# Spreading norm factors by transposes, a shorter wait behind the third f group, and an early word of weight tile two

## The chip, the cores and the metric

The kernel runs on one core of one Trainium2 chip. The metric is the device time in microseconds of one execution; a figure for a kernel is the median of several executions. All inputs and outputs are float32.

## The reference

The kernel computes a two-layer bidirectional encoder trunk over 256 tokens of width 2048. Sixteen learned meta tokens are put in front, so that every stage works on T = 272 tokens. Each layer does this:

```python
h = rmsnorm(x, norm_mix[i])                       # x * rsqrt(mean(x*x) + 1e-6) * g
q, k, v, f, ga, gf = split(h @ w_in[i])           # 1024, 256, 256, 1024, 2048, 2048 columns
q, k = rope_2d(rmsnorm(q, q_norm[i])), rope_2d(rmsnorm(k, k_norm[i]))   # per head of 128
attn = softmax(q @ k.T / sqrt(128)) @ v           # 8 heads, 2 key/value heads
four = real(fft2(f, axes=(positions, 128 channels of a group)))          # 8 groups, ortho
merged = sigmoid(ga + b) * (attn @ w_attn_br[i]) + sigmoid(gf + b) * (four @ w_four[i])
x = x + merged @ w_out[i]
h2 = rmsnorm(x, norm_ffn[i])
u_gate = dwconv3(h2 @ w_up_gate)                  # 5632 channels, 3 taps along the tokens
x = x + (silu(u_gate) * (h2 @ w_up_val)) @ w_down[i]
```

The meta tokens are dropped at the end. Two small quantities matter here: the norm factor of each token (one number for each of the 272 tokens, the reciprocal root of a mean of squares), and the same factor for each token and key head.

## The kernel before

**Data layout.** Activations are held with channels on the partitions and tokens along the free axis: `XT` is the residual stream, 16 blocks of 128 channels by 272 tokens. A factor per token must therefore be the same on all 128 partitions when it multiplies such a block. `rstdB` is that: 128 x 272, the norm factors spread over all partitions.

**Matmuls.** Each weight matrix is streamed in tiles of 128 x 1024 f32 (512 KB, tag `raw`). Each tile is split in two parts of the reduced format fp32r: the high part `wh` is a cast on ScalarE (L286) and the low part `wl` a subtraction on VectorE (L288). The activations are split in the same way (`xHL`; L501 and the operation behind it). A product is then three matmuls, high by high, high by low and low by high (L357 to L359 in `group`, L424 to L426 in `first_groups`). One group has 256 output channels: two accumulators in PSUM over 64 weight blocks of 128 x 128.

**The order of the work.** SP issues the loads of weight tiles in the order of a list, a few tiles ahead. TensorE runs through the groups. Everything that is not such a matmul (norms, the Fourier branch, attention, gates) is written as Python generators that are pushed on a list called `shadow`. After every second pair of weight blocks, `step()` resumes the first generator whose pause has run out; the number that a generator yields is its pause in steps. So `yield 4` puts at least four steps of matmuls between two parts of a side job on TensorE. `drain()` resumes the generators there and then until none is left, and `until(hold, flag)` does so until a flag is set. Within this order a scheduler places the instructions; the loads marked `keep_in_program_order`, and TensorE and VectorE inside `manual_schedule`, stay as written.

**The norm factors** (`norm_stats`). The sums of squares `acc` lie with one partial sum on each partition. Three transposes against an identity (L590, `ps_nst`) and a reduction give one number per token, with the tokens on the partitions: column 0 for the 16 meta tokens (repeated on all partitions), columns 1 and 2 for the two blocks of 128 tokens. A power of -1/2 on GpSimd gives `tok`, 128 x 3 (L497). To spread them, three VectorE operations multiply the columns into a constant mask of identities (`dg`, L600), and a plain f32 matmul with a matrix of ones (L603, `ps_nb`) sums over the partitions, so that every output partition holds all 272 factors; ScalarE copies them to `rstdB`. `kstats` does the same for each of the two key heads (`dk`, L966 `ps_kb`). `norm_stats` is run four times, `kstats` twice.

**The start.** GpSimd fills small tiles with constants; ScalarE's queue loads the norm gains `prm`; SP issues the first blocks of `XT` and of weight tile one (`raw0`) by turns. Weight tile two (`raw1`) is held back on purpose: a one-column copy on GpSimd reads the first block of `raw0` and writes `raw1`, and the load of `raw1` has to wait for that copy.

```python
nc.gpsimd.tensor_copy(raws[1][:, 0, 0:1], r0[:, 0, 0:1])                            # L469
tc.keep_in_program_order(nc.sync.dma_start(raws[1], chunks[1][0]))                  # L470
tc.keep_in_program_order(nc.sync.dma_start(XT[:, 4:8, :], xT[:, 4:8, :]))
```

Behind it SP issues tiles three and four (`load_raw`) and `XT` 8:12, and, after the first matmuls, `XT` 12:16 and a part of the constants.

**The f groups of layer 0.** The first two f groups run together (`first_groups`, `ps_f`), and beside them the generator `sums` forms the norm factors. It then evicts the two groups with `f_evac`: VectorE multiplies each accumulator by `rstdB` and folds the positions into `E` (L654, L655; the middle positions into `remE` and `remO`). Each eviction pushes a generator `f_chan(i)`, the transform over channels: four matmuls `ps_fa` (L674, L675) that read `E`, and the copies behind them. Then:

```python
ps = group((l, "f", 2), xr(0), T, "aux")
drain()
f_evac(2, ps)
...
f_evac(3, group((l, "f", 3), xr(0), T))
```

Of the kernel before, what the change touches and what calls it, by code (L numbers as in the profile page):

```python
# [76 lines left out]

C_COS, C_SIN, C_MASK = 0, T, 2 * T
C_ID = 3 * T
C_CC = C_ID + P  # L80
# [15 lines left out]
def _constants():  # L96
# [11 lines left out]
    eye = np.eye(P)  # L108
    m16 = (np.arange(P)[:, None] % NM == np.arange(NM)[None, :]) / (P // NM)
    mask = np.concatenate([m16, eye, eye], 1)  # L110
    j = np.arange(P)
# [14 lines left out]
    gm = (np.arange(P)[:, None] // NM == np.arange(NG)[None, :]).astype(np.float64)  # L126
    consts = np.concatenate([cos, sin, mask, eye, cc, sc, br, gm], 1).astype(f32)
    bmat = np.concatenate([b0, b1], 1).astype(f32)
# [27 lines left out]
def encoder_kernel(ctx, tc, xT, params, consts, bmat, cfold, csign, w_fl, w_f64c, w_in, w_abr, w_four, w_f64, w_out, w_up, w_down, w_vn, w_dn, w_dt, out):  # L156
# [163 lines left out]
    def drain():  # L320
        while shadow:
            step(True)
# [77 lines left out]
    def first_groups(pss):  # L400
# [4 lines left out]
        for kt in range(KT // CW * 2 * CW):  # L405
# [26 lines left out]
            if kt == 0:  # L432
                tc.keep_in_program_order(nc.sync.dma_start(XT[:, 12:16, :], xT[:, 12:16, :]))
                tc.keep_in_program_order(nc.sync.dma_start(cst[:, C_MASK:C_CC], consts[:, C_MASK:C_CC]))
            step()
# [7 lines left out]
    cst = per.tile([P, C_N], F32, name="cst")  # L443
    ones = per.tile([P, P], F32, name="ones")
    warm = per.tile([P, 1], F32, name="warm")
# [12 lines left out]
    small = ctx.enter_context(tc.tile_pool(name="small", bufs=4))  # L458

    nc.gpsimd.memset(mhalf, -0.5)  # L460
    nc.scalar.dma_start(prm[:, 0:P_BG], params[:, 0:P_BG])
# [13 lines left out]
    tc.keep_in_program_order(nc.sync.dma_start(XT[:, 8:12, :], xT[:, 8:12, :]))  # L475
    nc.gpsimd.memset(ones, 1.0)
    nc.gpsimd.memset(V3.bitcast(F32), 0.0)
# [6 lines left out]
    sin = cst[:, C_SIN:C_SIN + T]  # L484
    mask = cst[:, C_MASK:C_MASK + T]
    ident = cst[:, C_ID:C_ID + P]
# [70 lines left out]
    def weight_sums():  # L557
# [7 lines left out]
        for s_ in range(1, len(VSETS)):  # L565
# [6 lines left out]
            for q, base, more in kinds:  # L572
                for j in range(NV // 2 + 1):
# [3 lines left out]
                    if j:  # L577
                        issue(dst(q, j - 1), more(j - 1), accum_op=ALU.add, max_dma_last_dim=4096)
                        ready_sums.update((s_, q, 2 * j - 2 + k) for k in range(2))
                        yield 1  # L580

    def norm_stats(holder, gap=0):
        am = small.tile([P, P // NM, NM], F32, tag="am", name="am", bufs=1)
        nc.vector.tensor_copy(am, _rep(acc[:, 0:NM], P // NM))
        lhs = (am.rearrange("p a b -> p (a b)"), acc[:, 16:144], acc[:, 144:272])
        if gap:
            yield gap
        ps = psum.tile([P, 512], F32, tag="aux", name="ps_nst")
        for i in range(3):
            nc.tensor.transpose(ps[:, i * P:(i + 1) * P], lhs[i], ident)  # L590
        ms = small.tile([P, 3], F32, tag="ms", name="ms")
        nc.vector.tensor_reduce(ms, ps[:, 0:3 * P].rearrange("p (i n) -> p i n", i=3), axis=AX.X, op=ALU.add)
        nc.vector.tensor_scalar(ms, ms, 1.0 / D, EPS, op0=ALU.mult, op1=ALU.add)
        tok = small.tile([P, 3], F32, tag="tok", name="tok")
        pow_half(tok, ms)
        holder["tok"] = tok
        yield 4
        dg = small.tile([P, T], F32, tag="sq", name="dg", bufs=2)
        for i, (a, b) in enumerate(BLK):
            nc.vector.tensor_scalar(dg[:, a:b], mask[:, a:b], tok[:, i:i + 1], None, op0=ALU.mult)  # L600
        yield 2
        pb = psum.tile([P, 512], F32, tag="aux", name="ps_nb")
        nc.tensor.matmul(pb[:, :T], ones, dg, start=True, stop=True)  # L603
        nc.scalar.copy(rstdB, pb[:, :T])
        tok2 = small.tile([P, 3], F32, tag="tok2", name="tok2")
        nc.vector.tensor_tensor(tok2, tok, tok, op=ALU.mult)
        holder["tok2"] = tok2
# [4 lines left out]
    for l in range(DEPTH):  # L612
# [6 lines left out]
        with tc.tile_pool(name=f"mix{l}", bufs=1) as mp:  # L619
# [105 lines left out]
            if l == 0:  # L725
                def sums(pss):
                    for m in range(KT):
                        norm_sum(m)
                        yield 4 if m % 4 == 3 else 1
                    yield from norm_stats(hold, 4)  # L730
                    yield 3
                    for i in range(2):
                        f_evac(i, pss[i])
                        yield 2

                pss = []
                push(sums(pss), 4)
                first_groups(pss)
                for dst, src in ((cst[:, 0:C_MASK], consts[:, 0:C_MASK]), (cst[:, C_CC:], consts[:, C_CC:]), (prm[:, P_BG:], params[:, P_BG:])):
                    tc.keep_in_program_order(nc.sync.dma_start(dst, src))  # L740
# [3 lines left out]
                with tc.manual_schedule(engines={mybir.EngineType.PE, mybir.EngineType.DVE}):  # L744
                    ps = group((l, "f", 2), xr(0), T, "aux")
                drain()
                f_evac(2, ps)
# [203 lines left out]
            def kstats():  # L951
# [8 lines left out]
                for kv in range(NKV):  # L960
                    dk = ut("dk")
                    for i, (a, b) in enumerate(BLK):
                        nc.vector.tensor_scalar(dk[:, a:b], mask[:, a:b], rk[:, kv, i:i + 1], None, op0=ALU.mult)
                    yield 5
                    pk = psum.tile([P, 512], F32, tag="aux", name="ps_kb")
                    nc.tensor.matmul(pk[:, :T], ones, dk, start=True, stop=True)  # L966
                    nc.vector.tensor_tensor(kp[:, kv, :], kp[:, kv, :], pk[:, :T], op=ALU.mult)
# [606 lines left out]
```

## Time and profile before

| | before |
|---|---|
| device time, median of 3 runs | 2528.14 us (2527.78 to 2528.75) |
| the profiled execution: device time | 2528.75 us |
| its span in the trace | 2526.8 us (1.95 us lie around it) |
| TensorE (PE) busy | 2516.0 us, 100% of the span, 18848 matmuls |
| VectorE (DVE) busy | 1985.9 us, 79% |
| ScalarE (ACT) busy | 1343.6 us, 53% |
| GpSimd (POOL) busy | 205.7 us, 8% |
| moved by DMA | 706.85 MB, 280 GB/s in the mean |

The span runs from the first to the last instruction in the trace, and the device time has a little more around it. Busy times are times in which an engine runs at least one instruction; matmuls on TensorE overlap, so that a busy TensorE isn't idle, but a matmul's duration is not what it costs. In a row of the timeline the first number is the start in microseconds from the start of the span, the second the duration; then come the engine, the line of the kernel, the operation, the output and the inputs by their names in the program, the shapes, and in brackets the idle time ahead of it with what ended it. In a row of groups, three numbers with slashes are the shortest, the median and the longest duration in ns.

### The profile page before, as it was taken

The numbers are of one execution on the slowest core, as the hardware profiler recorded it, in microseconds if no ns is written. First come the engines' busy times: TensorE is split into PE (matmuls) and PEld (weight loads), VectorE is DVE, ScalarE is ACT, GpSimd is POOL, SyncE is SP. The second block draws the span as 40 slices with busy tenths as digits, with TensorE's granted clock in tenths as the row PEclk, the third lists the DMA queues.
The fourth block names the chain that finished last, engine by engine and source line by source line (L and its number), as shares of the span: only waits on it lengthen the run. The fifth ranks groups of instructions, "written<-read, shape, count | busy, mean of one in ns | idle before, by whom it ended". The sixth has DMA issues, their size and how long they took to land.

```text
span 2526.8 us, 47925 instructions
## 1 busy us (share of the span) xinstructions
PE 2516.0 (100%) x18848; PEld 2433.3 (96%) x18848; DVE 1985.9 (79%) x3151; ACT 1343.6 (53%) x1921; POOL 205.7 (8%) x393
## 2 busy tenths in 40 slices
PE   8999999999999999999999999999999999999999
PEld 8999999999999999999999999999988899998887
DVE  7687866778878667888768887666778787898898
ACT  5455434554444334444445555444676665666665
POOL 0000000012212222222200000000000000000000
PEclk9999999999999999999999999999999999999999
DMA  7545558879999999999975647888778887788887
GB/s 255 165 151 163 190 190 249 260 250 371 395 325 381 397 379 377 384 378 388 379 286 193 204 149 235 269 257 270 245 261 290 296 290 237 259 280 292 277 302 269
DMA packets 194770, 706.85 MB, mean 280 GB/s; under 512 B 22112, under 2 KB 27360, under 8 KB 194288
## 3 DMA queue, kind: packets, MB, share of 16 engines
q1 hardware_dynamic: 146768, 517.09, 59.2%
q0 software_dynamic: 46336, 184.57, 21.2%
q8 instruction: 147, 2.41, 0.4%
q10 hardware_dynamic: 1440, 2.13, 0.2%
q14 instruction: 79, 0.65, 0.1%
HBM read 623.32 MB, written 111.15 MB: 291 GB/s over the span
## 4 chain that ended last, share of the span: by engine, by line
PE 98%; DMA 1%; DVE 0%; ACT 0%; issue 0%; SPq 0%; POOL 0%; DVEq 0%; ACTq 0%
PE ps_p L1414 14%; PE ps_ug L359 7%; PE ps_ug L358 7%; PE ps_ug L357 7%; PE ps_d L358 4%; PE ps_uv L358 4%; PE ps_d L357 3%; PE ps_uv L359 3%; PE ps_d L359 3%; PE ps_uv L357 3%; PE ps_o L358 3%; PE ps_ga L358 2%; PE ps_gf L358 2%; PE ps_o L357 2%; PE ps_ga L359 2%; PE ps_o L359 2%
## 5 line engine op out<-in xcount | busy, mean ns | idle before, releaser
L286 ACT CAST wh<-raw 128x1024 fp32r<-128x1024 f32 (+1 forms) x961 | 999.8, 1046 | 905.8 <-PE ps_ug L358 213.5
L288 DVE TENSOR_TENSOR wl<-raw,wh 128x1024 fp32r<-128x1024 f32 (+1 forms) x961 | 1158.9, 1217 | 407.6 <-ACT wh L286 396.7
L358 PE MATMUL ps_ug<-xHL,wh 128*128 128x272 f32 (+1 forms) x1408 | 401.5, 285 | 0.0
L357 PE MATMUL ps_ug<-xHL,wh 128*128 128x272 f32 (+1 forms) x1408 | 400.8, 285 | 0.0
L359 PE MATMUL ps_ug<-xHL,wl 128*128 128x272 f32 (+1 forms) x1408 | 400.4, 286 | 0.0
L358 PEld LDWEIGHTS ps_ug<-xHL,wh 128*128 128x128 f32 x1408 | 264.7, 188 | 3.2
L357 PEld LDWEIGHTS ps_ug<-xHL,wh 128*128 128x128 f32 x1408 | 264.6, 188 | 3.2
L359 PEld LDWEIGHTS ps_ug<-xHL,wl 128*128 128x128 f32 x1408 | 264.0, 188 | 1.5 <-DVE wl L288 1.1
L1414 PE MATMUL ps_p<-wh,opnd 128*128 128x512 f32 x816 | 222.8, 393 | 0.0
L358 PE MATMUL ps_uv<-xHL,wh 128*128 128x272 f32 x704 | 203.3, 289 | 0.0
L358 PE MATMUL ps_d<-gHL,wh 128*128 128x272 f32 x704 | 202.9, 288 | 0.0
L357 PE MATMUL ps_d<-gHL,wh 128*128 128x272 f32 x704 | 202.9, 288 | 0.0
L359 PE MATMUL ps_uv<-xHL,wl 128*128 128x272 f32 x704 | 202.6, 288 | 0.0
L357 PE MATMUL ps_uv<-xHL,wh 128*128 128x272 f32 x704 | 202.3, 287 | 0.0
L359 PE MATMUL ps_d<-gHL,wl 128*128 128x272 f32 x704 | 202.1, 287 | 0.0
L1414 PEld LDWEIGHTS ps_p<-wh,opnd 128*128 128x128 f32 x816 | 148.4, 188 | 29.6 <-ACT wh L286 0.2
L357 PE MATMUL ps_ga<-xHL,wh 128*128 128x272 f32 (+1 forms) x512 | 147.8, 289 | 0.0
L518 DVE TENSOR_TENSOR wi<-wi,wi 128x512 f32<-128x512 f32 x224 | 147.0, 685 | 0.0
L357 PE MATMUL ps_gf<-xHL,wh 128*128 128x272 f32 (+1 forms) x512 | 146.8, 287 | 0.0
L358 PE MATMUL ps_o<-mL,wh 128*128 128x272 f32 (+1 forms) x512 | 146.5, 286 | 0.0
L358 PE MATMUL ps_ga<-xHL,wh 128*128 128x272 f32 (+1 forms) x512 | 146.1, 285 | 0.0
L359 PE MATMUL ps_o<-mH,wl 128*128 128x272 f32 (+1 forms) x512 | 146.1, 285 | 0.0
(378 smaller groups left out, 5965.7 us busy)
## 6 DMA issues: line engine op xcount, KB each, us to landing
raw<-in_w_up SPq DMA_DIRECT2D x288, 512.0 KB, 6.1
raw<-in_w_in SPq DMA_DIRECT2D x191, 512.0 KB, 4.2
raw<-in_w_down SPq DMA_DIRECT2D x88, 512.0 KB, 7.0
wi<-in_w_dn POOLq DMA_DIRECT2D x80, 512.0 KB, 9.3
ft<-wi POOLq DMA_DIRECT2D x80, 512.0 KB, 7.9
raw<-ft SPq DMA_DIRECT2D x80, 512.0 KB, 4.5
raw<-in_w_out SPq DMA_DIRECT2D x64, 512.0 KB, 4.3
raw<-fv SPq DMA_DIRECT2D x64, 512.0 KB, 4.6
```

Source lines behind the costliest of these rows:

```text
L286: nc.scalar.copy(h[:, a:b], r[:, a:b])
L288: nc.vector.tensor_tensor(lo[:, a:b], r[:, a:b], h[:, a:b].bitcast(F32), op=ALU.subtract)
L357: nc.tensor.matmul(o, h[:, c, sl], a, start=kt == 0, stop=False)
L358: nc.tensor.matmul(o, h[:, c, sl], b, start=False, stop=False)
L359: nc.tensor.matmul(o, lo[:, c, sl], a, start=False, stop=kt == nk - 1)
L518: tt = lambda *v, **kw: tc.keep_in_program_order(nc.vector.tensor_tensor(*v, **kw))
L1414: nc.tensor.matmul(ps[h], x, w[:, 512 * h:512 * h + 512], start=fresh and (s_, q) in BEGIN and first, stop=(s_, q) in END and end, skip_gr ...
```

## The change

There are three edits.

1. *Spread by transposes.* The new `spread(ps, cols)` makes three transposes on TensorE. Each takes one column of the factors, repeated 128 times along the free axis with a step of zero (no copy is made), and transposes it against the identity into 16 or 128 columns of PSUM; the result has the same row on every partition. It takes the place of `dg` and the matmul with ones in `norm_stats`, and of `dk` and its matmul in `kstats`. The pauses are kept (`yield 4` and `yield 2` become `yield 6`; in `kstats` both stay). The tile `ones` and its memset on GpSimd go, and so does the mask among the constants: the early load of constants has 128 columns in place of 400.
2. *The third f group.* `sums` sets a flag once the first two evictions are issued, and behind the third f group `until(hold, "evac")` takes the place of `drain()`. What `drain()` forced out at this place besides, the channel transforms of groups 0 and 1, is left to the steps of the fourth group.
3. *A word per partition of tile two.* The first instruction on GpSimd is now a load of 128 words, the first of each partition of weight tile two, into the first column of `remE`. Nobody reads them: the memset of `remE` writes over them. In the built program that memset has to wait until the words have landed, and it stands on GpSimd right ahead of the copy L469.

In the built program two more things move, by the scheduler and not by an edit: at the start of the last layer's feed-forward part some transposes of the residual stream stand ahead of `ps_nb`, and a few weight casts on ScalarE and folding steps of the weights change places with their neighbours.

```diff
--- before.py
+++ after.py
@@ -75,8 +75,8 @@
 TH = T // 2 + 2
 BLK = ((0, 16), (16, 144), (144, 272))
 
-C_COS, C_SIN, C_MASK = 0, T, 2 * T
-C_ID = 3 * T
+C_COS, C_SIN = 0, T
+C_ID = 2 * T
 C_CC = C_ID + P
 C_SC = C_CC + HC1
 C_BR = C_SC + HC1
@@ -106,8 +106,6 @@
     cos = np.concatenate([np.cos(ar), np.cos(ar), np.cos(ac), np.cos(ac)], 0)
     sin = np.concatenate([-np.sin(ar), np.sin(ar), -np.sin(ac), np.sin(ac)], 0)
     eye = np.eye(P)
-    m16 = (np.arange(P)[:, None] % NM == np.arange(NM)[None, :]) / (P // NM)
-    mask = np.concatenate([m16, eye, eye], 1)
     j = np.arange(P)
     ang = 2.0 * np.pi * ((j[:, None] * j[None, :]) % P) / P
     cc = (np.cos(ang) / math.sqrt(P))[:, :HC1]
@@ -124,7 +122,7 @@
     br[9:16, 1] = sl[129:136, :TH]
     br = np.tile(br.reshape(NM, 2 * TH), (NG, 1))
     gm = (np.arange(P)[:, None] // NM == np.arange(NG)[None, :]).astype(np.float64)
-    consts = np.concatenate([cos, sin, mask, eye, cc, sc, br, gm], 1).astype(f32)
+    consts = np.concatenate([cos, sin, eye, cc, sc, br, gm], 1).astype(f32)
     bmat = np.concatenate([b0, b1], 1).astype(f32)
     return np.ascontiguousarray(consts), np.ascontiguousarray(bmat)
 
@@ -431,7 +429,7 @@
                 pump(len(chunks))
             if kt == 0:
                 tc.keep_in_program_order(nc.sync.dma_start(XT[:, 12:16, :], xT[:, 12:16, :]))
-                tc.keep_in_program_order(nc.sync.dma_start(cst[:, C_MASK:C_CC], consts[:, C_MASK:C_CC]))
+                tc.keep_in_program_order(nc.sync.dma_start(cst[:, C_ID:C_CC], consts[:, C_ID:C_CC]))
             step()
 
 
@@ -441,7 +439,6 @@
     xH, xL = xHL[:, :, 0, :], xHL[:, :, 1, :]
     prm = per.tile([P, P_N], F32, name="prm")
     cst = per.tile([P, C_N], F32, name="cst")
-    ones = per.tile([P, P], F32, name="ones")
     warm = per.tile([P, 1], F32, name="warm")
     mhalf = per.tile([P, 24], F32, name="mhalf")
     BH = per.tile([P, 2, TH], F32R, name="BH")
@@ -457,6 +454,7 @@
     o64m = per.tile([P, P], F32, name="o64m")
     small = ctx.enter_context(tc.tile_pool(name="small", bufs=4))
 
+    nc.gpsimd.dma_start(remE[:, 0, 0:1], chunks[1][0][:, 0, 0:1])
     nc.gpsimd.memset(mhalf, -0.5)
     nc.scalar.dma_start(prm[:, 0:P_BG], params[:, 0:P_BG])
     nc.scalar.activation(warm, mhalf[:, 0:1], AF.Copy)
@@ -473,7 +471,6 @@
     load_raw(3)
     st["raw"] = 4
     tc.keep_in_program_order(nc.sync.dma_start(XT[:, 8:12, :], xT[:, 8:12, :]))
-    nc.gpsimd.memset(ones, 1.0)
     nc.gpsimd.memset(V3.bitcast(F32), 0.0)
     nc.gpsimd.memset(o64.bitcast(F32), 0.0)
     nc.gpsimd.memset(o64m, 0.0)
@@ -482,7 +479,6 @@
 
     cos = cst[:, C_COS:C_COS + T]
     sin = cst[:, C_SIN:C_SIN + T]
-    mask = cst[:, C_MASK:C_MASK + T]
     ident = cst[:, C_ID:C_ID + P]
     ccm = cst[:, C_CC:C_CC + HC1]
     scm = cst[:, C_SC:C_SC + HC1]
@@ -579,6 +575,11 @@
                         ready_sums.update((s_, q, 2 * j - 2 + k) for k in range(2))
                         yield 1
 
+    def spread(ps, cols):
+        for i, (a, b) in enumerate(BLK):
+            n = b - a
+            nc.tensor.transpose(ps[:, a:b], cols[0:n, i:i + 1].to_broadcast([n, P]), ident[0:n, 0:n])
+
     def norm_stats(holder, gap=0):
         am = small.tile([P, P // NM, NM], F32, tag="am", name="am", bufs=1)
         nc.vector.tensor_copy(am, _rep(acc[:, 0:NM], P // NM))
@@ -594,13 +595,9 @@
         tok = small.tile([P, 3], F32, tag="tok", name="tok")
         pow_half(tok, ms)
         holder["tok"] = tok
-        yield 4
-        dg = small.tile([P, T], F32, tag="sq", name="dg", bufs=2)
-        for i, (a, b) in enumerate(BLK):
-            nc.vector.tensor_scalar(dg[:, a:b], mask[:, a:b], tok[:, i:i + 1], None, op0=ALU.mult)
-        yield 2
+        yield 6
         pb = psum.tile([P, 512], F32, tag="aux", name="ps_nb")
-        nc.tensor.matmul(pb[:, :T], ones, dg, start=True, stop=True)
+        spread(pb, tok)
         nc.scalar.copy(rstdB, pb[:, :T])
         tok2 = small.tile([P, 3], F32, tag="tok2", name="tok2")
         nc.vector.tensor_tensor(tok2, tok, tok, op=ALU.mult)
@@ -732,18 +729,19 @@
                     for i in range(2):
                         f_evac(i, pss[i])
                         yield 2
+                    hold["evac"] = True
 
                 pss = []
                 push(sums(pss), 4)
                 first_groups(pss)
-                for dst, src in ((cst[:, 0:C_MASK], consts[:, 0:C_MASK]), (cst[:, C_CC:], consts[:, C_CC:]), (prm[:, P_BG:], params[:, P_BG:])):
+                for dst, src in ((cst[:, 0:C_ID], consts[:, 0:C_ID]), (cst[:, C_CC:], consts[:, C_CC:]), (prm[:, P_BG:], params[:, P_BG:])):
                     tc.keep_in_program_order(nc.sync.dma_start(dst, src))
                 bt = rt("bt")
                 bt = bt[:, :, :TH]
                 tc.keep_in_program_order(nc.sync.dma_start(bt, bmat.rearrange("p (a b) -> p a b", a=2)))
                 with tc.manual_schedule(engines={mybir.EngineType.PE, mybir.EngineType.DVE}):
                     ps = group((l, "f", 2), xr(0), T, "aux")
-                drain()
+                until(hold, "evac")
                 f_evac(2, ps)
                 nc.scalar.copy(BH, bt)
                 tc.keep_in_program_order(nc.vector.tensor_tensor(BL, bt, BH.bitcast(F32), op=ALU.subtract))
@@ -958,12 +956,9 @@
                 pow_half(rk.rearrange("p a b -> p (a b)"), kss.rearrange("p a b -> p (a b)"))
                 yield 6
                 for kv in range(NKV):
-                    dk = ut("dk")
-                    for i, (a, b) in enumerate(BLK):
-                        nc.vector.tensor_scalar(dk[:, a:b], mask[:, a:b], rk[:, kv, i:i + 1], None, op0=ALU.mult)
                     yield 5
                     pk = psum.tile([P, 512], F32, tag="aux", name="ps_kb")
-                    nc.tensor.matmul(pk[:, :T], ones, dk, start=True, stop=True)
+                    spread(pk, rk[:, kv])
                     nc.vector.tensor_tensor(kp[:, kv, :], kp[:, kv, :], pk[:, :T], op=ALU.mult)
                 yield 3
                 qs = swap(kp)
```

## The prediction

> **What bounds the kernel now.** I read the page first, then the waits of TensorE, then the timeline around each edited line.
>
> ```profile
> PE 2516.0 (100%) x18848; PEld 2433.3 (96%) x18848; DVE 1985.9 (79%) x3151; ACT 1343.6 (53%) x1921; POOL 205.7 (8%) x393
> ...
> PE 98%; DMA 1%; DVE 0%; ACT 0%; issue 0%; SPq 0%; POOL 0%; DVEq 0%; ACTq 0%
> ```
>
> TensorE is busy for 2516.0 of 2526.8 us and carries 98% of the chain that ended last. A microsecond counts only if it is taken out of TensorE's own stream or out of a wait of TensorE. The list of those waits is short (columns: us in total, times, longest):
>
> ```profile
> PE ps_f L424 <- ACT wh L286: 5.5, 2, 5.0
> PE ps_fa L675 <- ACT w L368: 1.0, 1, 1.0
> PE ps_uv L354 <- DVE wl L288: 0.7, 2, 0.4
> ```
>
> Of the 5.5 us, 5.0 are the wait for the first data and 0.5 the wait for weight tile two. So all that is idle after the start is about 2.2 us. VectorE at 79% and ScalarE at 53% are on the path nowhere else. That sets the scale: this change can gain some microseconds of TensorE's work and of these waits, not more. I take 0.2%, or 5.06 us of 2528.14, as about what a measurement of this kernel can tell from no change; an edit of 2 us lies inside it.
>
> **Part A, the spread by transposes.** Removed: four matmuls `ps_nb` and four `ps_kb` in plain f32 with 272 columns (each is two records), and 24 small VectorE operations (`dg`, `dk`). Added: 8 times 3 transposes of 16, 128 and 128 columns. A duration is no price on a pipelined engine; the price is how far the starts of the neighbours move apart.
>
> ```profile
> 35.01 0.29 PE L359 MATMUL ps_f<-xHL,wl 128*128 128x272 f32 x1
> 35.14 0.27 PE L590 MATMUL ps_nst<-cst,am 128*128 128x128 f32 x1
> 35.25 0.38 PE L590 MATMUL ps_nst<-cst,acc 128*128 128x128 f32 x2
> ...
> 35.59 0.29 PE L358 MATMUL ps_f<-xHL,wh 128*128 128x272 f32 x1
> ...
> 39.86 0.29 PE L359 MATMUL ps_f<-xHL,wl 128*128 128x272 f32 x1
> 39.99 0.62 PE L603 MATMUL ps_nb<-dg,ones 128*128 128x272 f32 x2
> ...
> 40.57 0.29 PE L358 MATMUL ps_f<-xHL,wh 128*128 128x272 f32 x1
> ```
>
> Undisturbed, neighbours start 0.125 us apart (39.86 and 39.99). Around `ps_nb` the starts of L359 and L358 are 0.71 us apart where two steps would be 0.25, so one f32 matmul costs 0.46 us. Around the three transposes of `ps_nst`, the nearest rows for the new ones (f32, against the same identity), they are 0.58 apart, so three cost 0.33 us, 0.11 each. The saving is 0.13 each time, 8 x 0.13 = 1.05 us. No row shows a stationary operand that is one column repeated, or a transpose of 16 columns. From below: if the short one costs nothing, the gain is 8 x 0.24 = 1.9 us. From above: if each costs its whole duration, there is a loss (a rival below). I take 1.05, the row of the same kind.
>
> ```profile
> L590 PE MATMUL ps_nst<-cst,acc x8: 272/272/273, 35.2 to 1825.3; 128*128 128x128 f32 x8
> ```
> ```profile
> L600 DVE TENSOR_SCALAR dg<-cst,tok x12: 233/279/394, 38.3 to 1828.9; 128x128 f32<-128x128 f32 x8, 128x16 f32<-128x16 f32 x4
> ```
> ```profile
> 36.51 1.80 POOL L497 TENSOR_TENSOR tok<-ms,mhalf 128x3 f32<-128x3 f32 x1 [32.31 <-DVE ms L593]
> ```
>
> The 24 VectorE operations of some 0.28 us are 6 us of an engine with slack: nothing. The new transposes wait for `tok` on POOL, ready at 38.31, and the pauses kept hold their place on TensorE (39.99), so that wait stays covered by 1.7 us. The constants load behind the first matmuls shrinks from 200 to 64 KB; none of TensorE's waits names it: nothing.
>
> **Part B, the third f group.** Before, `drain()` put the channel transforms of groups 0 and 1 (`ps_fa`) into TensorE's stream ahead of the fourth group's matmuls; one of them ran into VectorE.
>
> ```profile
> 44.96 0.33 PE L675 MATMUL ps_fa<-cst,E 128*128 128x65 f32 x2
> ...
> 46.23 0.29 PE L357 MATMUL ps_f<-xHL,wh 128*128 128x272 f32 x1
> 47.47 0.41 PE L675 MATMUL ps_fa<-cst,E 128*128 128x65 f32 x2 [0.96 <-ACT w L368]
> ```
> ```profile
> 46.91 0.42 DVE L654 TENSOR_TENSOR E<-ft 128x254 f32<-128x254 f32 x1
> 47.24 0.42 DVE L655 TENSOR_TENSOR E<-ft 128x256 f32<-128x256 f32 x1
> ```
>
> The starts are 1.24 us apart instead of 0.125: 1.1 us lost. The row names the cast on ScalarE, but what the transform reads is `E`, finished by L654 at 47.33, just before 47.47. With the wait for two evictions alone, the transforms are left to the fourth group's own steps: in the order of the changed program the first comes 24 matmuls later and the second 34 after that, so about 47.9 and 53. The first `E` was ready by 44.96, where its transform ran without a wait, the second is at 47.66, so neither waits. Their own work is unchanged. What is late next: the third eviction now stands ahead of them on VectorE, and one low-half split of the weights moves forward by about 3.5 us, before it is due. Taken: the whole 1.1 us. Its other end is 0, if the stall returns at another place.
>
> **Part C, a word per partition of tile two.** POOL now issues first of all a transfer of 128 words into `remE`; the memset of `remE` waits for its landing, and behind that memset stands the copy L469 that lets SP load weight tile two. Behind that load SP holds XT 4:8, tiles three and four, and XT 8:12, so any delay passes to all of them.
>
> ```profile
> 0.74 0.12 POOL L460 MEMSET mhalf<- 128x24 f32 x1 [0.29 <-POOLq L1566]
> ...
> 2.84 0.50 POOL L1011 MEMSET pn<- 128x128 f32 x3
> 4.02 0.18 POOL L469 COPY raw<-raw 128x1 f32<-128x1 f32 x1 [0.68 <-DMA raw<-in_w_in]
> ...
> 371.76 0.71 POOL L563 DMA_DIRECT2D fv<-in_w_vn  x1
> ```
> ```profile
> 4.23 5.44 DMA raw<-in_w_in
> ```
> ```profile
> 9.75 1.14 ACT L286 CAST wh<-raw 128x512 fp32r<-128x512 f32 x2 [1.23 <-DMA raw<-in_w_in]
> 11.24 1.76 ACT L501 ACTIVATE xHL<-XT,prm 128x272 fp32r<-128x272 f32 x4 [0.34 <-DMA XT<-in_xT]
> 12.91 1.13 ACT L286 CAST wh<-raw 128x512 fp32r<-128x512 f32 x2
> ```
> ```profile
> fv<-in_w_vn POOLq DMA_DIRECT2D x12, 6.6
> ...
> prm<-in_params ACTq DMA_DIRECT2D x1, 32.0 KB, 3.0
> ...
> raw<-in_w_in SPq DMA_DIRECT2D x191, 512.0 KB, 4.2
> ```
>
> When do the words land? The issue costs POOL 0.7 us (371.76 is its first transfer before). The early load of `prm`, 32 KB from ScalarE's queue, took 3.0 us to land; the slow end is 6.6, for POOL's own transfers of 1 MB. I take 3.0, since the words too move almost nothing, and add that 0.7: landed at 0.74 + 3.7 = 4.4. POOL's other memsets, 0.4 us later than now (0.7 less the memset of `ones` and the moved one, 0.14 each), end at 3.8 and hide most of it. Then the memset (0.2) and the copy (0.2): tile two is issued at 4.85 instead of 4.23. It then took 5.44 us, against a median of 4.2 for its group, which I put down to the loads ahead of it. At the median it lands at 9.05, earlier than now (9.67); at 5.44 it lands at 10.3, and TensorE loses 0.6. The touch of the same rows can only help between these. On the gain side the bound is the wait for tile two, 0.5 us in the waits (0.67 by the starts), and little of it can be kept: the next tile's cast at 12.91 stands behind four activations that wait for XT 4:8. Between +0.6 and -0.67 I take -0.1.
>
> By the Trainium skill (DMA: Bandwidth & Descriptors, section Anatomy of one DMA, SWDGE path) such a transfer has a fixed cost of about 2.0 us; as an estimate the words would land at 2.8 and the sum would be the same, with no delay at all. No run here shows it.
>
> **The last layer.** The order there changes a little: row transposes come ahead of `ps_nb`, and ScalarE's weight casts are spread otherwise. The waits there were 0.7 us (L354, above). ScalarE has one cast more (1.14 us by L286 above) queued ahead of another, so I count 0 and keep +1.1 for the range.
>
> **The sum.** -1.05 - 1.1 - 0.1 = -2.25 us. The profiled execution took 2528.75 us (span 2526.8 and 1.95 around it), 0.61 over the median of the three runs. It becomes 2526.5, and the median of 2528.14 becomes **2525.9 us**.
>
> **The rivals.**
> - *The words hold tile two* (slower than before; chance 0.1). If they land after 6.6 us, at 7.34, SP issues at 7.75, 3.5 us late, and with it all that stands behind on SP. TensorE then stands still after tile one for 3.5 us more: 2528.14 - 2.15 + 3.5 = 2529.5. It eats the other parts from a landing at 6.0 on: issued at 6.45, tile two lands after 5.44 us at 11.9, 2.2 later than now. For it: nothing but POOL's big transfers. Against: theirs are a megabyte.
> - *Transposes cost their duration* (slower; 0.04). Three times 0.272 us is 0.82 against 0.46: +0.36 x 8 = 2.9 instead of -1.05, so 2528.14 + 2.9 - 1.1 - 0.1 = 2529.8. Against: the same row starts every 0.11 us. The Trainium skill (TensorE: Matmul & The Clock Gate, Part 4: PE-mode transpose) gives about 275 ns for one in a kernel and would have the clock gate not count it as work. The trace agrees with the duration, 272, but not that it is the price.
> - *Tile two comes earlier and the next tile with it* (0.15). The whole 0.67 is kept: 2525.3.
> - *The stall of part B returns elsewhere* (0.1), so that the move of the transforms does not do what it says: 2527.0. For it: the two operations of `E` start 0.33 us apart and last 0.42, so VectorE is full there. Against: both `E` are done before their new places.
> - *The last layer's cast is late* (0.09): 1.1 us more there, 2527.0.
>
> **How the numbers follow.** The forecast keeps 0.52. Its own ends, a 16-column transpose that costs nothing (-0.85) and tile two late (+0.7), give 2525.0 to 2526.6. The range takes in the three rivals of the same sign, their sums with each other, and half a microsecond for the spread of single runs (2527.78 to 2528.75): 2524.0 to 2528.6. It leaves out the two slow rivals and the joint ends. Faster by over 0.2% needs 2523.08, where all gains at their ends (1.9 + 1.1 + 0.67) still fall short by 1.4: 0.05. Slower by over 0.2% needs 2533.2, both slow rivals at once: 0.02. Within: 0.93.
>
> **What would show each step.** The three transposes should move their neighbours apart by 0.33 us or less. The wait of `ps_fa` should be gone, with no wait of its size between 44 and 60 us. The copy L469 should start at 4.0 to 4.7, and TensorE's wait before 10.4 should be no longer than now. I am wrong if TensorE's waits in the first 15 us grow by over 1 us, if a spread costs over 0.46, or if the span changes where no edited line stands.

## The result, and the profile after

| | before | after |
|---|---|---|
| device time, median of 17 runs each | 2528.49 us (2527.17 to 2530.95) | 2533.01 us (2532.49 to 2535.55) |
| the profiled execution: device time, span | 2528.75, 2526.8 us | 2532.53, 2530.8 us |

The changed kernel is slower: ratio 1.0018, 95% interval 1.0011 to 1.0024, or 4.5 us. The forecast was 2525.9 us in a range of 2524.0 to 2528.6.

The first part of the page of the changed kernel, and its list of TensorE's waits (us in total, times, longest):

```profile
PE 2521.3 (100%) x18856; PEld 2439.4 (96%) x18856; DVE 1982.1 (78%) x3127; ACT 1343.1 (53%) x1921; POOL 204.5 (8%) x393
```
```profile
PE ps_f L422 <- ACT wh L284: 4.9, 2, 4.5
PE ps_uv L352 <- DVE wl L286: 0.3, 1, 0.3
PE ps_p L1409 <- ACT wh L284: 0.2, 1, 0.2
```

The waits fell from 7.2 to 5.4 us, and the wait of `ps_fa` is gone. Yet the span grew by 4.0: TensorE is busy for 5.3 us more, with eight records more. So the time isn't lost in a wait. Where it is lost shows when the two traces are laid side by side, matmul by matmul. At 60 us each matmul starts 1.2 us earlier than before. From there the lead melts: 0.8 us are left at 530 us, in the gate, up and value groups it turns into a lag (+0.5 at 846, +1.6 at 1207 us), in the `d` groups between nothing changes, and at 2489 us it is 3.7. No line of the diff stands there. The view of busy time by stretches shows it as well: in 260 us of the first layer's `ps_ug` and `ps_uv`, and in 100 us of its `ps_d` (columns: us, PE busy with its matmuls, granted clock, DMA share, GB/s). First the kernel before:

```profile
570.00:830.00 260.00, 260.00 (x2077) 1.00 0.98 368
860.00:960.00 100.00, 100.00 (x799) 1.00 1.00 386
```

and the changed kernel:

```profile
570.00:830.00 260.00, 260.00 (x2069) 1.00 0.97 367
860.00:960.00 100.00, 100.00 (x799) 1.00 1.00 383
```

TensorE is busy without a gap in all four, at the same granted clock. In the first stretch it gets through 2069 matmuls instead of 2077 (125.7 ns each instead of 125.2), in the second through the same 799.

Then the edited places. A spread in the timeline of TensorE, changed kernel (the answer to the rows at 39.86 to 40.57; start, duration):

```profile
39.74 0.29 PE L357 MATMUL ps_f<-xHL,wl 128*128 128x272 f32 x1
39.96 0.59 PE L581 MATMUL ps_nb<-cst,tok 16*128 16x16 f32 x3
40.30 0.37 PE L355 MATMUL ps_f<-xHL,wh 128*128 128x272 f32 x1
40.51 0.29 PE L356 MATMUL ps_f<-xHL,wh 128*128 128x272 f32 x1
```

The neighbours (L357 and L356) start 0.77 us apart, against 0.71 around the old matmul and 0.58 around `ps_nst`. The channel transforms moved, and their first matmuls stand in the same timeline without a wait:

```profile
47.95 0.33 PE L672 MATMUL ps_fa<-cst,E 128*128 128x65 f32 x2
...
51.85 0.33 PE L672 MATMUL ps_fa<-cst,E 128*128 128x65 f32 x2
```

And GpSimd's start in the timeline, with the row of the words' load from the list of DMA issues (KB, us from issue to landing):

```profile
1.29 0.73 POOL L457 DMA_DIRECT2D remE<-in_w_in  x1 [0.84 <-POOLq L1561]
...
5.15 0.20 POOL L477 MEMSET remE<- 128x128 f32 x1 [0.81 <-DMA remE<-in_w_in]
5.30 0.17 POOL L467 COPY raw<-raw 128x1 f32<-128x1 f32 x1
```
```profile
remE<-in_w_in POOLq DMA_DIRECT2D x1, 0.5 KB, 3.8
```

### The profile page after: what moved, and what is told of

The parts are those of the page before. It is cut to its first block, busy times and chain, and to the rows that moved or that the text cites. A ratio compares the mean times of both kernels' runs of the same rounds, so it can differ in the third digit from the quotient of the medians.

```text
span 2530.8 us, 47907 instructions
## 1 busy us (share of the span) xinstructions
PE 2521.3 (100%) x18856; PEld 2439.4 (96%) x18856; DVE 1982.1 (78%) x3127; ACT 1343.1 (53%) x1921; POOL 204.5 (8%) x393
## 4 chain that ended last, share of the span: by engine, by line
PE 99%; DVE 0%; ACT 0%; DMA 0%; issue 0%; SPq 0%
PE ps_p L1409 14%; PE ps_ug L356 7%; PE ps_ug L357 7%; PE ps_ug L355 7%; PE ps_uv L355 4%; PE ps_d L356 4%; PE ps_uv L356 3%; PE ps_uv L357 3%; PE ps_d L355 3%; PE ps_d L357 3%; PE ps_gf L355 2%; PE ps_o L356 2%; PE ps_gf L356 2%; PE ps_ga L356 2%; PE ps_ga L355 2%; PE ps_ga L357 2%
## 5 line engine op out<-in xcount | busy, mean ns | idle before, releaser
L286 DVE TENSOR_TENSOR wl<-raw,wh 128x1024 fp32r<-128x1024 f32 (+1 forms) x961 | 1158.5, 1217 | 410.4 <-ACT wh L284 399.1
L356 PE MATMUL ps_ug<-xHL,wh 128*128 128x272 f32 (+1 forms) x1408 | 402.0, 286 | 0.0
L357 PE MATMUL ps_ug<-xHL,wl 128*128 128x272 f32 (+1 forms) x1408 | 400.3, 285 | 0.0
L356 PEld LDWEIGHTS ps_ug<-xHL,wh 128*128 128x128 f32 x1408 | 265.0, 188 | 3.1
L357 PEld LDWEIGHTS ps_ug<-xHL,wl 128*128 128x128 f32 x1408 | 264.8, 189 | 1.1 <-DVE wl L286 0.6
L356 PE MATMUL ps_uv<-xHL,wh 128*128 128x272 f32 x704 | 203.0, 288 | 0.0
L356 PE MATMUL ps_d<-gHL,wh 128*128 128x272 f32 x704 | 202.9, 288 | 0.0
L357 PE MATMUL ps_uv<-xHL,wl 128*128 128x272 f32 x704 | 202.7, 288 | 0.0
L357 PE MATMUL ps_d<-gHL,wl 128*128 128x272 f32 x704 | 202.1, 287 | 0.0
L355 PE MATMUL ps_gf<-xHL,wh 128*128 128x272 f32 (+1 forms) x512 | 147.4, 288 | 0.0
L356 PE MATMUL ps_o<-mL,wh 128*128 128x272 f32 (+1 forms) x512 | 146.6, 286 | 0.0
L356 PE MATMUL ps_gf<-xHL,wh 128*128 128x272 f32 (+1 forms) x512 | 146.2, 286 | 0.0
L356 PE MATMUL ps_ga<-xHL,wh 128*128 128x272 f32 (+1 forms) x512 | 146.2, 286 | 0.0
```

Of the source, the lines that this page charges most:

```text
L286: nc.vector.tensor_tensor(lo[:, a:b], r[:, a:b], h[:, a:b].bitcast(F32), op=ALU.subtract)
L355: nc.tensor.matmul(o, h[:, c, sl], a, start=kt == 0, stop=False)
L356: nc.tensor.matmul(o, h[:, c, sl], b, start=False, stop=False)
L357: nc.tensor.matmul(o, lo[:, c, sl], a, start=False, stop=kt == nk - 1)
```

## The experiments

**What else differs.** The instructions of the `ps_ug` groups are the same in both kernels; their operands lie elsewhere. Without `ones` (512 bytes per partition) and the mask (1088), every tile allocated behind them moved down, the weight tiles `wh` and `wl` and `gHL` by 1600 bytes. `xHL` lies ahead of them and did not move. So the distance from `xHL` to the weights changed, and that from `gHL` to the weights did not. Theory P says that this distance sets how soon matmuls follow one another, and that it counts modulo 256 bytes. Theory I puts it down to the instructions: the transposes, the eight records more, the order in the last layer.

The first four kernels add bytes per partition to a small tile ahead of the weight tiles and change no instruction. Their expectations name the place of `wh` itself modulo 256 (160 before, 96 after, 32); `xHL` begins at 128, so these are the distances 32, 224 and 160 of the table below.

```diff
-    o64m = per.tile([P, P], F32, name="o64m")
+    o64m = per.tile([P, P + 16], F32, name="o64m")[:, :P]   # 64 bytes; + 48: 192; + 64: 256
```

After, 64 bytes:

> The changed kernel with 64 bytes per partition added ahead of the weight tiles; instructions and their order stay the same. Theory P (places in the on-chip memory): the change freed 1600 bytes ahead of the weight tiles, so that wh and wl moved against xHL, and each matmul of xHL starts some 0.6 ns (272 columns) to 1.5 ns (258 columns) later after its neighbour; summed over the groups about +5.5 us. If only the distance modulo 256 bytes counts, 64 bytes put it back (1600 = 6 x 256 + 64): 2533.0 - 5.5 = about 2527.5. Theory I (the instructions themselves: the transposes, the order in the last layer, eight more records): nothing changes, 2533.0.

After, 192 bytes:

> The changed kernel with 192 bytes added at the same place: wh at 32 modulo 256 instead of 160 (before) or 96 (after). Theory P: xHL has its rows at 0 and 128 equally often, so that 32 and 160 should cost nearly the same: 2527 to 2529. Theory I: 2533.0.

Before, 192 bytes:

> The kernel before with 192 bytes added ahead of the weight tiles, not one instruction changed: wh at 96 modulo 256, as in the changed kernel. Theory P: 2528.5 + 5.5 = about 2534.0, with ps_ug of the first layer at 125.9 ns from start to start instead of 125.3. Theory I: 2528.5.

Before, 256 bytes:

> A control: the kernel before with 256 bytes added. Theory P with a period of 256 bytes: no change, 2528.5. If it is the absolute place or a longer period that counts, the time moves, by up to 5 us either way. Theory I: 2528.5.

A fifth one moves `xHL` as well:

```diff
-    xf = per.tile([P, KT * 2 * T + 8], F32R, name="xHL")
-    xHL = xf[:, :KT * 2 * T].rearrange("p (k r t) -> p k r t", k=KT, r=2)
+    xf = per.tile([P, KT * 2 * T + 24], F32R, name="xHL")
+    xHL = xf[:, 16:16 + KT * 2 * T].rearrange("p (k r t) -> p k r t", k=KT, r=2)
```

> The changed kernel with the 64 bytes put at the head of xHL instead of behind it: xHL and the weight tiles both move by 64, their distance stays that of the changed kernel, the weight tiles lie at the same addresses as in after_pad64. If the distance between the data that a matmul streams and its weights counts: about 2533. If the place of the weight tiles alone counts (their own alignment): about 2527.7, as after_pad64.

The columns of the next table: the distance from block 0 of `xHL` to the first weight tile modulo 256 (the blocks are 2176 bytes apart, so every second one has 128 more or less); the mean time from one matmul's start to the next one's, in ns, for matmuls that stream 272 and 258 columns of `xHL` and 272 of `gHL`, worked out from all pairs of the trace that have no wait or plain f32 matmul between them (some 6,830, 3,970 and 2,110); the median, and its ratio to the kernel before, measured beside it.

| kernel | distance | xHL 272 | xHL 258 | gHL 272 | median, us | ratio (95%) |
|---|---|---|---|---|---|---|
| before | 32 | 125.28 | 119.45 | 125.53 | 2528.49 | |
| after | 224 | 125.78 | 120.25 | 125.52 | 2533.01 | 1.0018 (1.0011 to 1.0024) |
| after_pad64 | 32 | 125.30 | 119.46 | 125.53 | 2527.68 | 0.9998 (0.9989 to 1.0007) |
| after_pad192 | 160 | 125.42 | 119.36 | 125.53 | 2526.19 | 0.9994 (0.9986 to 1.0003) |
| before_pad192 | 224 | 125.77 | 120.22 | 125.52 | 2533.53 | 1.0021 (1.0012 to 1.0030) |
| before_pad256 | 32 | 125.28 | 119.46 | 125.53 | 2528.03 | 1.0001 (0.9992 to 1.0010) |
| after_x64 | 224 | 125.78 | 120.23 | 125.52 | 2533.48 | 1.0020 (1.0011 to 1.0029) |

The kernel before turns into the slow one by 192 bytes (the same view):

```profile
570.00:830.00 260.00, 260.00 (x2069) 1.00 0.98 367
860.00:960.00 100.00, 100.00 (x800) 1.00 1.01 381
```

and the changed one loses its slowness by 64:

```profile
570.00:830.00 260.00, 260.00 (x2078) 1.00 0.98 369
860.00:960.00 100.00, 100.00 (x799) 1.00 1.01 388
```

In after_x64 the weight tiles lie where they lie in after_pad64, but `xHL` went along:

```profile
570.00:830.00 260.00, 260.00 (x2068) 1.00 0.98 366
860.00:960.00 100.00, 100.00 (x799) 1.00 1.01 386
```

So theory P holds in its direction in all five. In size it missed once: after_pad192 came 0.8 us below its range, and by the starts this is not the doing of `xHL` but of the matmuls that stream weights (512 columns), which take 2.0 us less than in after_pad64. Theory I falls in the three kernels for which it forecast another time than P (after_pad64, after_pad192, before_pad192); before_pad256 and after_x64 cannot part the two. What after_x64 parts is distance and place. It is the distance, not the place of the weights; 1600 bytes, 1600 less 64 that make it whole, and 192 in the other direction act by their rest modulo 256; and `gHL`, which kept its distance, kept its time to 0.01 ns. That two reads of the on-chip memory get in each other's way, the streamed data and the next weights, would fit this, but no run shows it.

**The parts alone.** In these the weight tiles lie where they lay before; A_only and A_full have 1600 bytes added for that. A_only is the kernel before with `spread`, without `ones` and the mask, and with:

```diff
-    o64m = per.tile([P, P], F32, name="o64m")
+    o64m = per.tile([P, P + 400], F32, name="o64m")[:, :P]
```

> Part A alone (spread by transposes), with 1600 bytes added ahead of the weight tiles so that they lie exactly where they lay before. By the starts in the changed kernel's trace a spread costs 0.52 us of TensorE against 0.46 before: 8 x 0.06 = +0.5 and about 2528.8. By the prediction's step (0.33 each): -1.05 and 2527.2.

```diff
-            n = b - a
-            nc.tensor.transpose(ps[:, a:b], cols[0:n, i:i + 1].to_broadcast([n, P]), ident[0:n, 0:n])
+            nc.tensor.transpose(ps[:, (0, 16, 144)[i]:(128, 144, 272)[i]], cols[:, i:i + 1].to_broadcast([P, P]), ident)
```

(A_full against A_only.)

> As A_only, but the first transpose of each spread takes all 128 rows (the factors of the 16 meta tokens are repeated on all partitions) and writes 128 columns, of which the second one writes over all but 16. Theory R (the change to 16 rows and back is what costs, since the loads around it aren't done ahead): the neighbours' starts 0.58 us apart as around ps_nst, so 0.33 a spread, and 1.5 us less than A_only: about 2527.2. Theory Z (a column repeated with step zero is slow to load): 0.77 us apart as in A_only, the same time.

```diff
-                drain()
+                until(hold, "evac")
```

(B_only against the kernel before, with the flag set in `sums`.)

> Part B alone (the third f group awaits the two evictions, no drain). If the 1.1 us between 46.23 and 47.47 were a wait of TensorE that nothing takes over: 2528.3 - 1.1 = about 2527.2 and no wait of ps_fa. If the stall returns later: 2528.3.

```diff
+    nc.gpsimd.dma_start(remE[:, 0, 0:1], chunks[1][0][:, 0, 0:1])
     nc.gpsimd.memset(mhalf, -0.5)
```

(C_only against the kernel before.)

> Part C alone (the words of tile two into remE ahead of everything on GpSimd). In the changed kernel the words landed at 5.1 us and the copy ran at 5.30 instead of 4.02; TensorE began 0.5 us earlier, waited for tile two all the same and was 0.1 us ahead at 15 us. So -0.1: about 2528.2. If the late tile two costs what its delay is: +1.3, 2529.6.

| kernel | median, us (before 2528.28) | ratio (95%) |
|---|---|---|
| A_only | 2527.71 | 0.9997 (0.9989 to 1.0006) |
| A_full | 2528.03 | 0.9998 (0.9989 to 1.0007) |
| B_only | 2528.88 | 1.0000 (0.9992 to 1.0009) |
| C_only | 2528.61 | 0.9999 (0.9991 to 1.0008) |

None can be told from the kernel before; intervals of some 2 us either way settle no dispute over 1 us. What they settle stands in the traces. A spread in the timeline of TensorE, A_full:

```profile
39.65 0.29 PE L357 MATMUL ps_f<-xHL,wl 128*128 128x272 f32 x1
39.78 0.49 PE L579 MATMUL ps_nb<-cst,tok 128*128 128x128 f32 x3
40.02 0.37 PE L355 MATMUL ps_f<-xHL,wh 128*128 128x272 f32 x1
40.23 0.29 PE L356 MATMUL ps_f<-xHL,wh 128*128 128x272 f32 x1
```

0.58 us from L357 to L356, as around `ps_nst`, and 0.77 in A_only: theory R holds and theory Z falls. A column repeated with step zero costs nothing; the transpose of 16 rows and 16 columns costs 0.19 us. A_full changes its rows and its columns together. The trace of the kernel before has matmuls that part them, in the last layer: plain f32 ones of 16 rows with 130 columns, between such of 128 rows (two records each).

```profile
1415.00 0.28 PE L359 MATMUL ps_q<-xHL,wl 128*128 128x258 f32 x1
1415.12 0.38 PE L872 MATMUL ps_fa<-cf,E 128*128 128x130 f32 x2
1415.43 0.48 PE L873 MATMUL ps_fa<-sg,e 16*128 16x130 f32 x2
1415.85 0.49 PE L874 MATMUL ps_fa<-cf,E 128*128 128x130 f32 x2
```

The two records of L872 start 0.11 us apart. From the second of them to the last of L874 the starts are 0.20 to 0.22 apart. So TensorE is also slow around 16 rows when the stream is long.

In the profiled execution of A_full a new wait takes 1.0 of the 1.5 us, since the scheduler orders VectorE otherwise in the last layer. The row of it in the list of TensorE's waits, A_full:

```profile
PE ps_f L844 <- DVE wl L286: 1.0, 1, 1.0
```

**The wait of ps_fa.** It is in the profiled runs of before and before_pad256 (1.2 and 1.3 us from start to start), but not in that of before_pad192, which has the same instructions, nor in those of C_only, A_only and A_full, which have the `drain()` too. So it comes and goes from one execution to the next. The timeline of ScalarE shows by what (in brackets the idle time and what ended it). Before:

```profile
39.69 0.85 ACT L752 CAST br<-cst 32x276 fp32r<-32x276 f32 x2 [3.43 <-DMA cst<-in_consts]
40.56 1.05 ACT L286 CAST wh<-raw 128x1024 fp32r<-128x1024 f32 x1
41.52 0.41 ACT L748 CAST BH<-bt 128x276 fp32r<-128x276 f32 x1
41.84 0.38 ACT L604 COPY rstdB<-ps_nb 128x272 f32<-128x272 f32 x1
```

and before_pad192:

```profile
38.02 0.86 ACT L752 CAST br<-cst 32x276 fp32r<-32x276 f32 x2 [2.29 <-DMA cst<-in_consts]
...
40.17 0.38 ACT L604 COPY rstdB<-ps_nb 128x272 f32<-128x272 f32 x1
```

`ps_nb` starts at 39.99 and at 39.45. On ScalarE a weight cast (`wh`, L286) and the copy to `rstdB` both stand behind a cast that waits for constants. Where these start 1.7 us later, both are 1.7 us late. VectorE's timeline shows which of the two held it up. Before:

```profile
41.65 1.23 DVE L288 TENSOR_TENSOR wl<-raw,wh 128x1024 fp32r<-128x1024 f32 x1 [2.68 <-ACT wh L286]
42.86 0.78 DVE L650 TENSOR_TENSOR ft<-ps_f,rstdB 128x272 f32<-128x272 f32 x2
```

and before_pad192:

```profile
39.98 1.23 DVE L288 TENSOR_TENSOR wl<-raw,wh 128x1024 fp32r<-128x1024 f32 x1 [1.54 <-ACT wh L286]
41.19 0.78 DVE L650 TENSOR_TENSOR ft<-ps_f,rstdB 128x272 f32<-128x272 f32 x2
```

VectorE waits for the weight cast, and the first eviction (L650) stands behind the subtraction that needs it. By then `rstdB` has been there for 0.6 us in both. In the two executions with the wait the eviction starts 2.9 us behind `ps_nb`, in the four without it 1.2 to 1.7. late_br puts the two casts behind the copy, which sets the weight cast free as well:

```diff
-        nc.scalar.copy(rstdB, pb[:, :T])
+        tc.keep_in_program_order(nc.scalar.copy(rstdB, pb[:, :T]))
...
-                nc.scalar.copy(BH, bt)
+                tc.keep_in_program_order(nc.scalar.copy(BH, bt))
...
-                    nc.scalar.copy(br3[a:a + 32], brem[a:a + 32])
+                    tc.keep_in_program_order(nc.scalar.copy(br3[a:a + 32], brem[a:a + 32]))
```

> The kernel before with two casts (br3 and BH, which wait for constants) put behind the copy to rstdB on ScalarE; TensorE's instructions and all addresses are the same. Theory S: the wait of ps_fa (1.1 us in the profiled run before, none in before_pad192, where the constants came 1.7 us earlier) comes from rstdB standing behind these casts, not from VectorE being full: rstdB is copied within 0.7 us of ps_nb, no wait of ps_fa is left, and executions that had it are about 1.1 us shorter: median 2527.3 to 2528.3. Theory V (VectorE is full there, as the prediction had it): the wait stays, 2528.3.

Its median is 2527.58 (before 2528.42; ratio 0.9997, 0.9989 to 1.0006), and in its timeline of ScalarE `rstdB` waits for nothing but `ps_nb`:

```profile
40.30 0.39 ACT L604 COPY rstdB<-ps_nb 128x272 f32<-128x272 f32 x1 [1.03 <-PE ps_nb L603]
```

There is no wait of `ps_fa` in its profile, as theory S has it, and the eviction starts 1.1 us behind `ps_nb`. The edit does not part the weight cast from `rstdB`, and it was the weight cast that VectorE waited for. One profile of a wait that comes and goes is little, and the time doesn't tell; the order on ScalarE is shown, its share in the median is not.

**A version that beats both.** Given the table, the distance can be chosen.

> after_pad192 with the transposes of all 128 rows from A_full: 8 x (0.77 - 0.58) = 1.5 us less of TensorE, so 2526.2 - 1.5 = about 2524.7. If the 0.19 a spread is hidden behind something in this kernel: 2526.2.

Measured 2526.04 us (ratio 0.9990, 0.9981 to 0.9999): the 1.5 us are saved at the spreads, and the same new wait of 1.0 us as in A_full takes most of it, so that the time can't be told from that of after_pad192. Then the blocks of `xHL` were put at one distance, with the casts as in late_br:

```diff
-    xf = per.tile([P, KT * 2 * T + 8], F32R, name="xHL")
-    xHL = xf[:, :KT * 2 * T].rearrange("p (k r t) -> p k r t", k=KT, r=2)
+    xf = per.tile([P, KT * (2 * T + 32)], F32R, name="xHL")
+    xHL = xf.rearrange("p (k v) -> p k v", k=KT)[:, :, :2 * T].rearrange("p k (r t) -> p k r t", r=2)
...
-    o64m = per.tile([P, P], F32, name="o64m")
+    o64m = per.tile([P, P + 56], F32, name="o64m")[:, :P]
```

> mended192 with the blocks of xHL 2304 instead of 2176 bytes apart, so that all 16 lie at the same place modulo 256 and not at two by turns, and with the weight tiles set so that the distance is the better of the two that the kernel before has by turns (160; 104 in the last layer); also with the casts that wait for constants put behind rstdB on ScalarE, as in late_br. From the starts of matmuls by distance in the traces so far, three matmuls of a weight block take 375.0 ns at this distance against 376.2 in the mean of after_pad192 (272 columns, some 2240 blocks) and 357.6 against 358.1 (258 columns, some 1750): -2.8 and -0.8 us, so about 2521, and 2520 to 2521 with what the casts give. If only the mean over all distances counts and not each block's own: 2524.7.

Measured 2520.78 us, ratio to the kernel before 0.9971 (0.9960 to 0.9981). The starts are 124.57 ns apart with 272 columns and 118.89 with 258, and the view by stretches shows it:

```profile
570.00:830.00 260.00, 260.00 (x2090) 1.00 0.98 372
860.00:960.00 100.00, 100.00 (x799) 1.00 1.01 384
```

2090 matmuls against 2077 before and 2069 in the changed kernel. That the forecast came to within a microsecond is in part luck. It started from 2524.7, where mended192 took 2526.04, and the distances were worth 5.3 us instead of 3.6: by the pairs of starts the matmuls of `xHL` gained 7.5 (three of 272 columns take 373.7 ns, not 375.0), and those that stream weights lost 2.1.

## Why the prediction was wrong

**The term that was missing.** The sum had only edited instructions in it and took every other matmul at its old price. The removed tiles were counted as work ("the memset of `ones`", "64 instead of 200 KB"), not as places. Worked out from the pairs of starts that both traces have, the moved tiles cost +3.4 us at the 272-column matmuls of `xHL`, +3.1 at those of 258, +0.3 at its 512- and 256-column ones, and -1.7 elsewhere (-1.1 at those that stream weights, -0.4 at `q`): +5.1 in all. Between before and before_pad256 the same reckoning gives -0.2. The prediction named the right sign of its own failure, a span that changes where no edited line stands, and gave it no chance. A second of its signs came true as well, a spread that costs over 0.46.

**Part A, mis-sized by 1.5 us.** Forecast 0.33 a spread, measured 0.52 (0.77 less the two steps of 0.125): eight of them cost +0.5 instead of saving 1.05. The step that failed is "the nearest row". `ps_nst` has 128 rows in all three transposes; for the short one the prediction bounded the price by nothing and by its whole duration, and then took that of `ps_nst` for it, though no row showed a transpose of 16 rows. The rows of L873 above, 16 rows in the trace before, were the nearer ones, and they are slow. The Trainium skill (TensorEngine Tiling (Array Packing), section Tiling Modes, Key Properties) says that a change of the tiling mode drains TensorE. The traces agree (in the built program the 16-row transpose has a tile of 32 x 128, its neighbours 128 x 128): the 16-row transpose starts 0.22 us after its neighbour instead of 0.125, the two behind it 0.16 apart instead of 0.11, and with 128 rows all of that is gone. By the rule the sum of part A would have had to allow a loss. The rival by which every transpose costs its duration was rightly low: three of 128 rows cost 0.33.

**Part B, right in the profile and not to be seen in the median.** The transforms run at 47.95 and 51.85 (forecast 47.9 and 53) without a wait, and nothing of that size came in its place. But the cause was misread. VectorE does the same work without a gap in executions that have no wait; in the profiled one it began 1.7 us later, since the weight cast that it needed stood on ScalarE behind a cast that waits for constants. That makes the wait a matter of when constants land. The 1.1 us are in two of the six profiled executions that have the `drain()` (late_br aside), and the sum booked them in full to the median.

**Part C, its size right by luck.** Forecast: words landed at 0.74 + 3.7 = 4.4, copy by 4.7. Measured: the transfer takes 3.8, but its row begins only at 1.29, so 5.1; the copy ran at 5.30. So it was 0.6 us later than the forecast's, and 1.28 later than before, and SP issued tile two at 5.50 instead of 4.23. It cost nothing, by the good case of the prediction's own reckoning, in which the transfer is shorter. The cast that waits for tile two ran at 9.44 instead of 9.75, changed kernel:

```profile
9.44 1.14 ACT L284 CAST wh<-raw 128x512 fp32r<-128x512 f32 x2 [0.82 <-DMA raw<-in_w_in]
```

So the transfer took at most 3.9 us instead of 5.44 (in C_only 4.08). Whether that is due to the words or to the loads ahead of it, no run parts. TensorE does not wait for tile two any more, other than the expectation of C_only has it; its second wait, 0.45 us at 6.67, is for a cast of tile one. The lead at 15 us is 0.1, as forecast. But the first matmul came 0.5 us earlier, and in before_pad192, before_pad256 and B_only, where no words are loaded, 0.4 to 0.6 earlier; at 15 us these three lie from 0.45 ahead of the kernel before to 1.8 behind it. Single profiles of the start differ by more than this part is worth.

**The last layer** gained some 0.35 us instead of 0. With -0.1 for the start, -1.1 for B in this pair of executions and +0.5 for A that makes -1.05, and with the +5.1 about +4.0. The spans differ by 4.0 too, but 0.3 of that lie behind the last matmul; so the parts are good to some 0.3 us.

**The chances.** None of the rivals was what happened; the two on the slow side were worked out at 2529.5 and 2529.8, and their mechanisms did not occur. The range held every cost of an edit and none of a side effect.

## What to carry to other kernels

Removing a buffer is an edit of every address behind it. Where TensorE is busy all the time, compare the matmuls that get done in equal stretches before looking for waits; if the count differs at the same clock in stages that nobody edited, look at what moved. Before crediting an edit with a wait that it takes away, see in a second profile whether the wait is always there.

## What the runs showed of the hardware

- The time from one matmul to the next depends on the distance between the streamed rows and the weights modulo 256 bytes: 124.57 to 125.78 ns on average with 272 columns, 118.89 to 120.25 with 258, in kernels with the same matmuls. By single distances the spread is wider: `wh` with 272 columns of `xHL` takes 124.5 ns at 32 and 96 and 127.2 at 160 and 224 in the changed kernel, but 124.95 at 32 and 124.45 at 160 in the kernel before. So a matmul's own distance does not settle its time; what else counts, the neighbours' distances or something else, is not shown.
- The Trainium skill (SBUF — State Buffer, section SBUF: two separate sides) has TensorE wait for no one at that memory. The measured times differ between layouts by 1% all the same, with the granted clock at 1.00 throughout.
- A transpose of 16 rows and 16 columns between matmuls of 128 rows costs 0.19 us more than one of 128 rows (0.77 against 0.58 for the three). Plain f32 matmuls of 16 rows and 130 columns start 0.20 to 0.22 us apart, where the two records of the 128-row one ahead of them are 0.11 apart. A column repeated with step zero costs no more than a full operand.
